# Input projection of a two-branch layer: seven block products of 2x2 blocks, in sweeps over pairs of column tiles

## Chip, core and metric

The kernel runs on one core of a Trainium2 chip. The metric is the device time of one execution in microseconds. In what follows PE is TensorE's matmul side, PEld its weight loads, DVE VectorE, ACT ScalarE, POOL GpSimd, SP SyncE (here it only issues DMAs).

## What is computed

One layer with two token mixers over a prompt of 1024 tokens and 8 samples of 8 tokens (1088 token columns), model width 2048, in float32:

```python
mod = silu(c) @ w_ada + b_ada
shift, scale, gate = split(mod, 3)
h = rms_norm(x, norm_gain) * (1 + scale) + shift
u_a, z_a, q, k, v, z_b, g_lr, m_a, m_b = split(h @ w_in, SPLIT_POINTS)
a_y, sa_re, sa_im = s5_branch(u_a, ...)          # diagonal complex state space, then a gated product with w_glu
a_out = (a_y * silu(z_a)) @ w_a_out
log_a = log_sigmoid(g_lr @ w_gate_up + b_gate) / 16
b_y, s_gla = gla_branch(q * DK ** -0.5, k, v, log_a, s0, head_gain)   # gated linear attention (GLA)
b_out = (b_y * silu(z_b)) @ w_b_out
merged = sigmoid(m_a) * a_out + sigmoid(m_b) * b_out
y = rms_norm(x + gate * (merged @ w_out), final_norm_gain)
```

`h @ w_in` is the input projection: 2048 rows by 72 column tiles of 128, and 16 further columns for `g_lr`.

## The kernel before

Activations lie with channels on partitions and tokens in the free dimension, as 16 k tiles of [128, 1088]. Every float32 operand of a large product is split into two parts (hi, lo), and a product is three matmuls: hi by hi, hi by lo, lo by hi (`mm3`, L69 to L71). Weights come in quarters of 4 k tiles, [128, 512]: SP loads the raw quarter (L52), ACT makes hi (L54), DVE makes lo (L56); six buffers each of hi and lo.

`product` (L73) walks the column tiles. For each of three token chunks (320, 384, 384 columns) it does 16 k steps of three matmuls into one PSUM bank and then calls an eviction function. Within it, `next(self.steps)` emits a piece of background work: first all of S5 (`s5_run`, L568: a setup of small DVE operations, then 16 units), later all of the GLA (`gla_run`, L733: four units of samples, 16 units of prompt). Evictions read PSUM on ACT (L601, L635, L644, L656), so the projection asks DVE for nothing but lo.

The program starts with the conditioning product (`ada_chunk`, L183: 16 chunks of 2 MB of `w_ada`), the norm of x, and `modulate` (L245), which gives hi and lo of h for one k tile; all 32 tiles of h then stay in SBUF until the projection is over. The first three column tiles go side by side over k (`product_k`, L91), two k tiles at a time, as soon as those two tiles of h are there, between the ada chunks. S5 runs beside column tiles 3 to 7 and those that follow, the GLA beside tiles 40 to 71, and eight last ada chunks (`ada_gates`, L956, with buffers of their own) beside tiles 8 to 15 and 32 to 39. Then come `branch_a` (w_glu), `merge` (w_a_out and w_b_out) and `final` (w_out).

The order in which each engine gets its instructions is set when the program is built: the framework's scheduler takes what the generators emit and orders each engine's queue by a simulated timeline. On the chip each queue runs in that order. A prompt unit of the GLA (`gla_unit`, L756) is one long chain: log gates (ACT with changes of its function table, DVE scans), seven levels of decays and scores (L814 to L842), the outputs and the state update (L932 to L941), and the norm (L945 to L953) with a DVE reciprocal (L133). Its scratch tile `t1` has one buffer: the norm at the end of a unit uses it, and so does the first step of the next unit (L778).

## Time and profile before

| | |
|---|---|
| time, median of 3 runs (range) | 2951.68 us (2951.25 to 2954.08) |
| span of the profiled execution | 2947.8 us |
| PE busy | 98% |
| DVE, ACT, POOL busy | 46%, 32%, 9% |
| granted TensorE clock, mean | 0.994 of full |
| DMA | 376.59 MB, mean 128 GB/s |

The page gives one profiled execution, engine by engine; a PE that is busy need not be at its peak, since matmuls overlap in the record. The run's own times lie 3.5 to 6.3 us above the profiled span (the median 3.9 us above). Busy shares are means over stages with different limits, so the stages are read by windows.

### The profile page before, as it was taken

How to read it: one execution, taken by the hardware profiler on the slowest of the kernel's cores; microseconds unless marked ns; L12 is line 12 of the kernel's file. 1: busy time of each engine (PE TensorE's matmuls, PEld its weight loads, DVE VectorE, ACT ScalarE, POOL GpSimd, SP SyncE). 2: the span in 40 equal slices, each digit the busy share in tenths (PEclk: the TensorE clock that was granted, in tenths of full speed). 3: DMA queues.
4: the chain of work that ended last, by engine and by line, in shares of the span. 5: the costliest groups of instructions: out<-in, count | busy, mean ns of one | idle time of the engine just before them, and what ended most of it. 6: DMA issues, size and time to landing. Idle time of an engine off the chain costs nothing.

```text
span 2947.8 us, 49487 instructions
## 1 busy us (share of the span) xinstructions
PE 2890.1 (98%) x19584; PEld 2762.2 (94%) x19584; DVE 1344.5 (46%) x3424; ACT 941.1 (32%) x1735; POOL 263.4 (9%) x430
## 2 busy tenths in 40 slices
PE   7999999999999999999999999999999999999988
PEld 3799999999989999999999999999999999899988
DVE  3587778751234444444453111114662233556455
ACT  4222222222234434443443111422232111444434
POOL 0002122210000000000000000301010000203021
PEclk9999999999999999999999999999999999999999
DMA  9634444442232222222223344423274333555455
GB/s 377 242 117 122 120 128 117 128 123 75 85 126 100 84 83 72 85 80 77 81 86 105 98 146 132 115 76 102 97 231 136 112 114 116 191 164 181 145 173 168
DMA packets 221881, 376.59 MB, mean 128 GB/s; under 512 B 35153, under 2 KB 111729, under 8 KB 219473
## 3 DMA queue, kind: packets, MB, share of 16 engines
q1 hardware_dynamic: 159856, 256.26, 26.8%
q0 software_dynamic: 24720, 75.59, 8.4%
q10 hardware_dynamic: 37072, 41.59, 4.1%
q8 instruction: 154, 2.52, 0.3%
q14 instruction: 79, 0.64, 0.1%
HBM read 288.44 MB, written 76.51 MB: 124 GB/s over the span
## 4 chain that ended last, share of the span: by engine, by line
PE 67%; DMA 2%; DVE 1%; ACT 1%; issue 1%; POOL 0%; DVEq 0%; ACTq 0%; POOLq 0%
PE mm L71 20%; PE mm L69 20%; PE mm L70 20%; DMA wraw<-in_w_out_dram 1%; DMA bz<-zbs 1%; PE bg L831 1%; PE bg L69 1%; PE bg L71 1%; PE bg L70 1%; PE bg L201 1%; PE bg L939 0%; PE bg L940 0%; PE bg L932 0%; DMA mx<-mscr 0%; DVE wlo L56 0%
## 5 line engine op out<-in xcount | busy, mean ns | idle before, releaser
L69 PE MATMUL mm<-hh,whi 128*128 128x384 f32 (+1 forms) x3360 | 1101.3, 329 | 4.2 <-ACT hh L264 4.2
L71 PE MATMUL mm<-hh,wlo 128*128 128x384 f32 (+2 forms) x3360 | 1103.0, 329 | 0.0
L70 PE MATMUL mm<-hl,whi 128*128 128x384 f32 (+1 forms) x3360 | 1100.0, 328 | 2.4 <-DVE hl L266 2.4
L56 DVE TENSOR_TENSOR wlo<-wraw,whi 128x512 fp32r<-128x512 f32 x560 | 406.1, 729 | 634.7 <-ACT whi L54 627.2
L69 PEld LDWEIGHTS mm<-hh,whi 128*128 128x128 f32 x3360 | 630.5, 188 | 19.2 <-issue 10.0
L70 PEld LDWEIGHTS mm<-hl,whi 128*128 128x128 f32 x3360 | 630.6, 188 | 10.1 <-DVE hl L266 3.6
L71 PEld LDWEIGHTS mm<-hh,wlo 128*128 128x128 f32 x3360 | 630.5, 188 | 5.5 <-issue 2.8
L54 ACT ACTIVATE whi<-wraw 128x512 fp32r<-128x512 f32 x560 | 351.3, 630 | 771.8 <-PE mm L70 561.6
L69 PE MATMUL mm<-ahi,whi 128*128 128x384 f32 (+3 forms) x1656 | 542.0, 328 | 13.4 <-DVE y L1084 10.4
L71 PE MATMUL mm<-ahi,wlo 128*128 128x384 f32 (+3 forms) x1656 | 542.2, 328 | 2.9 <-DVE wlo L56 2.9
L70 PE MATMUL mm<-alo,whi 128*128 128x384 f32 (+3 forms) x1656 | 541.6, 327 | 0.0
L69 PEld LDWEIGHTS mm<-ahi,whi 128*128 128x128 f32 x1656 | 313.5, 189 | 17.1 <-issue 11.0
L71 PEld LDWEIGHTS mm<-ahi,wlo 128*128 128x128 f32 x1656 | 313.5, 189 | 4.8 <-DVE wlo L56 3.5
L70 PEld LDWEIGHTS mm<-alo,whi 128*128 128x128 f32 x1656 | 313.6, 189 | 1.1
L635 ACT ACTIVATE ev<-mm 128x384 f32<-128x384 f32 (+1 forms) x120 | 55.9, 466 | 237.4 <-PE mm L71 234.4
L1042 DVE TENSOR_TENSOR m<-m,mm 128x384 f32<-128x384 f32 (+1 forms) x96 | 50.5, 529 | 146.9 <-PE mm L71 146.9
L645 DVE TENSOR_TENSOR ev<-ev,mm 128x384 f32<-128x384 f32 (+1 forms) x45 | 23.8, 530 | 181.3 <-ACT ev L644 181.2
L946 POOL TENSOR_TENSOR on<-on 128x256 f32<-128x256 f32 (+1 forms) x20 | 13.1, 653 | 961.3 <-ACT on L945 961.3
L644 ACT ACTIVATE ev<-mm 128x384 f32<-128x384 f32 (+1 forms) x45 | 21.1, 468 | 176.5 <-PE mm L71 176.3
L1040 ACT ACTIVATE m<-m 128x1088 f32<-128x1088 f32 x32 | 35.6, 1113 | 119.3 <-DMA m<-mbs 91.3
L480 POOL DMA_DIRECT2D tm<-kd x128 | 65.0, 516 | 43.0 <-DMA kd<-kk 18.8
L991 POOL DMA_DIRECT2D yt<-y x64 | 34.1, 540 | 380.1 <-ACT m L207 259.6
(334 smaller groups left out, 2580.6 us busy)
## 6 DMA issues: line engine op xcount, KB each, us to landing
wraw<-in_w_in_dram SPq DMA_DIRECT2D x288, 256.0 KB
wraw<-in_w_out_dram SPq DMA_DIRECT2D x192, 256.0 KB
adaraw<-in_w_ada_dram SPq DMA_DIRECT2D x64, 512.0 KB
gateraw<-in_w_ada_dram SPq DMA_DIRECT2D x16, 1024.0 KB
x<-in_xT_dram SPq DMA_DIRECT2D x16, 544.0 KB
m<-mas POOLq DMA_DIRECT2D x16, 544.0 KB, 4.9
m<-mbs POOLq DMA_DIRECT2D x16, 544.0 KB, 5.0
mscr<-m POOLq DMA_DIRECT2D x16, 544.0 KB, 3.1
```

The lines of the kernel that those rows point to most:

```text
L54: nc.scalar.activation(hi, raw, AF.Copy)
L56: nc.vector.tensor_tensor(lo, raw, hi.bitcast(F32), ALU.subtract)
L69: nc.tensor.matmul(ps, hi[:, c], ah[:, sl], start=start, stop=False)
L70: nc.tensor.matmul(ps, hi[:, c], al[:, sl], start=False, stop=False)
L71: nc.tensor.matmul(ps, lo[:, c], ah[:, sl], start=False, stop=stop)
L201: self.nc.tensor.matmul(ps[i:i + 32, :256], self.c32[:, k, :], raw[:, (k - k0) * 256:(k - k0 + 1) * 256], start=k < 4, stop=k >= KT - 4, t ...
L480: nc.gpsimd.dma_start(tm[16 * s:16 * s + 16], kd[0:16, :, 16 * (7 - s):16 * (7 - s) + P])
L635: nc.scalar.activation(e[:, :n], ps[:, :n], AF.Copy, scale=scale)
L831: nc.tensor.matmul(o, gs, blk(gs, w)[:, :, m:w], start=True, stop=True, tile_position=(0, 32 * i))
L991: nc.gpsimd.dma_start(yv[r:r + 16], self.yscr[2 * i + uu][:, g, :].rearrange("(t h) c -> h t c", h=16))
L1040: nc.scalar.activation(st["m"], st["m"], AF.Sigmoid)
L1042: V.tensor_tensor(mm, mm, ps[:, :n], ALU.mult)
```

## The change

The product of a pair of column tiles is written in 2x2 blocks: two halves of the k range, the two column tiles of the pair, and two halves of the tokens (544 each), and done with seven block products instead of eight (Winograd's form of Strassen's scheme). `SWEEPS` names the left operand (weights, or sums and differences of weight blocks) and the right operand (h, or sums and differences of blocks of h). 36 pairs stand in four groups of nine; within a group the kernel sweeps seven times over the nine pairs, one product per pair and sweep. Here one product of one pair is called a slot: 8 k tiles, two halves of 272 columns, three matmuls each, into two PSUM banks; there are two such buffers of two banks.

- Left operands (`left`): SP loads [128, 1024] blocks (tag `raw`, five buffers); for s1 to s4 POOL adds or subtracts two blocks; s1 and s2 are also written to DRAM and read back. ACT makes hi, DVE lo (three buffers each).
- Right operands: seven sets of 8 tiles, kept in DRAM. The first set and the second are made at the start (`blocks_first`, `blocks_second`), t1 too; t2, t3, t4 and 22 in the first group, as background (`blocks_sums`). Each further sweep reads its 8 tiles from DRAM (`right`), one per slot, into 16 buffers (two sets).
- Results: the first sweep's product goes to a tile by ACT; in all others DVE adds PSUM to it, once or twice per slot (288 additions of 544 columns). Finished quarters leave through four buffers (`fin`) by POOL's queue.
- Start: the ada chunks come first as a whole, then the sweeps. Background work: `blocks_sums` in the first group; then `behind`: S5 with one step per slot, the GLA with three, and `ada_gates`, whose raw tiles now come from the five `raw` buffers that the weight blocks use.

```diff
+    SWEEPS = (("a11", "11"), ("a12", "21"), ("s1", "t1"), ("s2", "t2"), ("s3", "t3"), ("a22", "t4"), ("s4", "22"))
+    def left(self, w, a, pair, scr):
...
+            raw = self.wx.tile([P, H], F32, tag="raw", name="araw", bufs=5)
+            nc.sync.dma_start(raw, src)
...
+        def both(x, y, op):
+            nc.gpsimd.tensor_tensor(x, x, y, op)
+            return x
...
+        elif a == "s1":
+            x = both(blk(j2, 0), blk(j2, 1), ALU.add)
+            nc.gpsimd.dma_start(scr[0], x)
+        elif a == "s2":
+            x = both(load(scr[0]), blk(j1, 0), ALU.subtract)
+            nc.gpsimd.dma_start(scr[1], x)
+        elif a == "s3":
+            x = both(blk(j1, 0), blk(j2, 0), ALU.subtract)
+        else:
+            x = both(blk(j1, 1), load(scr[1]), ALU.subtract)
+        hi = self.wi.tile([P, H], F32R, tag="whi", name="ahi", bufs=3)
+        nc.scalar.activation(hi, x, AF.Copy)
+        lo = self.wi.tile([P, H], F32R, tag="wlo", name="alo", bufs=3)
+        nc.vector.tensor_tensor(lo, x, hi.bitcast(F32), ALU.subtract)
...
+    def sweep_group(self, w, group, first, last, tail=None):
...
+        for r, (an, bn) in enumerate(self.SWEEPS):
...
+            for i, (pair, s, final) in enumerate(group):
+                hi, lo = self.left(w, an, pair, self.sscr[pair])
+                ps = self.psum2()
+                for k in range(8):
+                    c = slice(k * P, (k + 1) * P)
+                    for m in range(2):
+                        o = ps[:, m, :NC]
+                        bh, bl = B[k][:, m * NC:(m + 1) * NC], B[k][:, HT + m * NC:HT + (m + 1) * NC]
+                        nc.tensor.matmul(o, hi[:, c], bh, start=k == 0, stop=False)
+                        nc.tensor.matmul(o, hi[:, c], bl, start=False, stop=False)
+                        nc.tensor.matmul(o, lo[:, c], bh, start=False, stop=k == 7)
+                    if k in self.ticks:
+                        next(self.steps, None)
+                next(coming, None)
...
+                if r == 0:
+                    nc.scalar.activation(two(x), v, AF.Copy, scale=s)
+                elif r == 1:
+                    out(0, 0, x)
+                elif r == 2:
+                    add(y, x)
+                elif r == 3:
+                    add(x, x)
+                    add(y, y)
+                elif r == 4:
+                    add(x, x)
+                    out(1, 1, y)
+                elif r == 5:
+                    out(1, 0, x, -1)
+                else:
+                    out(0, 1, y)
...
-            for k in range(0, KT, 8):
-                raw = self.gp2.tile([P, 2048], F32, tag="raw", name="gateraw", bufs=3)
...
+            for k in range(0, KT, 4):
+                raw = self.wx.tile([P, 1024], F32, tag="raw", name="gateraw", bufs=5)
...
+    def behind(self):
+        self.s5ctx = ExitStack()
+        self.ticks = (3,)
+        yield from self.s5_run()
+        self.s5ctx.close()
+        self.ticks = (1, 4, 6)
+        gla = ExitStack()
+        self.gla_pool(gla)
+        yield from self.gla_run()
+        gla.close()
+        yield from self.ada_gates()
...
+        self.ticks = (2, 5)
+        self.steps = self.blocks_sums()
+        for g in range(4):
+            self.sweep_group(w, pairs[9 * g:9 * g + 9], g == 0, g == 3)
+            if g == 0:
+                for _ in self.steps:
+                    pass
+                su.close()
+                self.steps = self.behind()
+                next(self.steps)
```

What the change moves on the engines' queues stands below at three places (names as in the trace: `mm` is a product's PSUM tile, `bg` one of the background work).

**PE, start.** Before, among the ada chunks (L201) the first column tiles (L69 to L71) already run:

```order
L201 MATMUL bg<-adaraw,c_210 32x256 x12
L69 MATMUL mm<-hh,whi 128x384
L69 MATMUL mm<-hh,whi 128x320
L201 MATMUL bg<-adaraw,c_210 32x256 x4
L70 MATMUL mm<-hl,whi 128x384
L71 MATMUL mm<-hh,wlo 128x384
```

With the change (ada is L336 and L344, the sweeps are L167 to L169):

```order
L344 MATMUL bg<-ident,m 128x128 x2
L336 MATMUL bg<-adaraw_1148,c_283 32x256 x4
L336 MATMUL bg<-adaraw_1154,c_283 32x256 x4
L336 MATMUL bg<-adaraw_1160,c_283 32x256 x4
L344 MATMUL bg<-ident,m 128x128 x2
L167 MATMUL mm<-b_543,ahi 128x272
L168 MATMUL mm<-b_543,ahi 128x272
L169 MATMUL mm<-b_543,alo 128x272
```

Every ada matmul now stands ahead of the first matmul of the projection.

**PE, GLA.** Before, where one prompt unit ends (L949) and the next begins (L775), projection matmuls stand on both sides, and so at each step of each unit:

```order
L69 MATMUL mm<-hh,whi 128x320
L70 MATMUL mm<-hl,whi 128x320
L949 MATMUL bg<-on,ones_h 128x256
L775 MATMUL bg<-gr,wgu 128x256
L801 MATMUL bg<-q,k 32x32 x8
L71 MATMUL mm<-hh,wlo 128x320
L69 MATMUL mm<-hh,whi 128x320
```

With the change, at the end of the sixth sweep of the last group (L1163 ends a unit, L989 begins one):

```order
L167 MATMUL mm<-bt_22230,ahi 128x272
L168 MATMUL mm<-bt_22230,ahi 128x272
L169 MATMUL mm<-bt_22230,alo 128x272
L1163 MATMUL bg<-on,ones_h 128x256
L989 MATMUL bg<-gr,wgu 128x256
L1015 MATMUL bg<-q,k 32x32 x8
L1045 MATMUL bg<-g 32x16 x40
L1054 MATMUL bg<-g 32x32 x4
L1054 MATMUL bg<-g 64x64 x2
L1086 MATMUL bg<-ident,kd 128x128 x2
L1146 MATMUL bg<-v,kT 128x256 x2
```

Seven whole prompt units stand there one behind the other with no matmul of a sweep between them; the last of them and the first matmuls of the seventh sweep:

```order
L1154 MATMUL bg<-q,St_16190 128x128
L1163 MATMUL bg<-on,ones_h 128x256
L336 MATMUL bg<-gateraw,c_283 32x256 x16
L344 MATMUL bg<-ident,m 128x128 x2
L336 MATMUL bg<-gateraw,c_283 32x256 x8
L167 MATMUL mm<-b_22455,ahi 128x272
L168 MATMUL mm<-b_22455,ahi 128x272
```

Before those seven, the prompt units stand among the sweeps, about six slots to a unit. On SP's queue the second weight block that the seventh sweep's first pair needs stands behind the loads and stores of the same seven units.

**DVE, S5's setup.** Before, no eviction of the projection is on DVE. With the change, in the second sweep of the second group, the addition of the first pair's product (L187) is followed by 157 rows of S5 (its setup, the tables and scans of its first units) and three of lo, and then by that of the second pair; the end of the stretch:

```order
L693 TENSOR_TENSOR rt<-rot,par 128x8
L694 TENSOR_TENSOR rot<-rot,rt 128x4x2
L695 TENSOR_TENSOR rot<-rot,rt 128x4x2
L691 TENSOR_TENSOR rot<-rot,par 128x8x4
L692 TENSOR_TENSOR rt<-rot,par 128x16
L693 TENSOR_TENSOR rt<-rot,par 128x16
L694 TENSOR_TENSOR rot<-rot,rt 128x4x4
L187 TENSOR_TENSOR fin<-pt,mm 128x544
```

Before, rows of this kind stand between two of lo, and no matmul waits for them; now an addition that frees a PSUM buffer stands behind them.

## Rows read from the trace of the kernel before

**Rows 1.** The page: busy time of each engine, and the chain that ended last.

```profile
PE 2890.1 (98%) x19584; PEld 2762.2 (94%) x19584; DVE 1344.5 (46%) x3424; ACT 941.1 (32%) x1735; POOL 263.4 (9%) x430
...
PE 67%; DMA 2%; DVE 1%; ACT 1%; issue 1%; POOL 0%; DVEq 0%; ACTq 0%; POOLq 0%
```

**Rows 2.** Busy time by windows (us, PE, PEld, DVE, ACT, POOL busy, PE clock, DMA share, GB/s).

```profile
10.00:20.00 10.00, 10.00 (x46) 3.75 (x45) 0.00 (x0) 8.32 (x8) 0.00 (x0) 1.00 1.02 415
...
400.00:500.00 100.00, 100.00 (x661) 98.09 (x660) 77.26 (x295) 22.73 (x53) 22.36 (x44) 1.00 0.43 127
1200.00:1400.00 200.00, 200.00 (x1680) 192.79 (x1668) 88.77 (x259) 79.71 (x172) 3.68 (x5) 1.00 0.25 79
```

**Rows 3.** PE timeline, 384 columns (start, length, what).

```profile
1699.41 0.33 PE L69 MATMUL mm<-hh,whi 128*128 128x384 f32 x1
...
1700.28 0.34 PE L71 MATMUL mm<-hh,wlo 128*128 128x384 f32 x1
```

**Rows 4.** PE timeline, 320 columns.

```profile
1702.10 0.31 PE L69 MATMUL mm<-hh,whi 128*128 128x320 f32 x1
...
1703.26 0.31 PE L71 MATMUL mm<-hh,wlo 128*128 128x320 f32 x1
```

**Rows 5.** PE timeline, 256 columns.

```profile
2871.73 0.28 PE L71 MATMUL mm<-ahi,wlo 128*128 128x256 f32 x1
...
2872.91 0.28 PE L69 MATMUL mm<-ahi,whi 128*128 128x256 f32 x1
```

**Rows 6.** Line L69 on PE, to 200 us (ns min/median/max, first and last start).

```profile
L69 PE MATMUL bg<-hh,whi x48: 358/368/496, 59.5 to 168.7; 128*128 128x448 f32 x32, 128*128 128x512 f32 x16
```

**Rows 7.** DMA issues of the page's sixth part (count, KB each).

```profile
adaraw<-in_w_ada_dram SPq DMA_DIRECT2D x64, 512.0 KB
...
x<-in_xT_dram SPq DMA_DIRECT2D x16, 544.0 KB
```

**Rows 8.** Lines L71 and L775 on PE, 1200 to 1400 us.

```profile
L71 PE MATMUL mm<-hh,wlo x344: 307/334/444, 1200.1 to 1399.9; 128*128 128x384 f32 x116, 128*128 128x320 f32 x56
...
L775 PE MATMUL bg<-gr,wgu x5: 468/471/471, 1228.5 to 1395.3; 96*128 96x256 f32 x5
```

**Rows 9.** ACT timeline, the start of one prompt unit.

```profile
1233.33 0.46 ACT L778 ACTIVATE t<-bg 128x256 f32<-128x256 f32 x1
...
1236.83 0.51 ACT L780 ACTIVATE t<-t,one 128x256 f32<-128x256 f32 x1
```

**Rows 10.** DVE timeline, the norm of one unit.

```profile
1229.47 1.74 DVE L133 RECIPROCAL rsn<-t 128x256 f32<-128x256 f32 x1
...
1232.95 0.69 DVE L953 TENSOR_TENSOR on<-bg,rsn 128x512 f32<-128x512 f32 x1
```

**Rows 11.** DVE and ACT groups by shape (busy us, mean ns, idle before them).

```profile
L814 DVE TENSOR_TENSOR d<-b 128x256 f32<-128x256 f32 x112 | 43.5, 418 | 0.5
L1042 DVE TENSOR_TENSOR m<-m,mm 128x384 f32<-128x384 f32 x64 | 35.1, 551 | 113.2 <-PE mm L71 113.2
L817 DVE TENSOR_TENSOR g<-d,k 128x128 f32<-128x128 f32 x112 | 31.8, 284 | 0.0
...
L1046 DVE TENSOR_TENSOR m<-m 128x1088 f32<-128x1088 f32 x16 | 20.5, 1283 | 0.0
...
L815 ACT ACTIVATE d<-d 128x128 f32<-128x128 f32 x112 | 34.3, 306 | 17.2 <-DVE d L814 17.1
```

**Rows 12.** Lines L1131 and L977 on DVE and POOL (ns min/median/max, first and last start).

```profile
L1131 POOL TENSOR_TENSOR y<-y,rs x12: 1982/2438/2777, 2691.4 to 2850.0; 128x832 f32<-128x832 f32 x12
L1131 DVE TENSOR_TENSOR y<-y,bg x6: 677/678/686, 2938.4 to 2941.4; 128x512 f32<-128x512 f32 x6
L1131 DVE TENSOR_TENSOR y<-y,rs x4: 1026/2808/2814, 2691.3 to 2843.1; 128x832 f32<-128x832 f32 x4
...
L1131 POOL TENSOR_TENSOR y<-y,rc x2: 1263/1264/1264, 2938.4 to 2939.6; 128x512 f32<-128x512 f32 x2
...
L977 DVE TENSOR_TENSOR alo<-mx,ahi x11: 1276/1278/4007, 2511.5 to 2549.3; 128x1088 fp32r<-128x1088 f32 x11
```

More of the change, by code (lines that the diff above doesn't have):

```diff
@@ L29 @@
 QK4 = 512
+HT = T // 2
+NC = HT // 2
 class Hybrid:
@@ L234, in norm_in @@
-        tmp = self.act(F32, "rt")
-        for c, (t0, n) in enumerate(CH):
-            part = self.ep.tile([P, 416], F32, tag="ev", name="part", bufs=3)
-            nc.scalar.activation(part[:, :n], pss[c][:, :n], AF.Copy)
-            pss[c] = self.psum(False)
-            nc.tensor.matmul(pss[c][:, :n], ones_32, part[:, :n], start=True, stop=True)
-            nc.scalar.activation(tmp[:, t0:t0 + n], pss[c][:, :n], AF.Ln, bias=self.eps)
+            if k < KT // 2:
+                nc.scalar.activation(sq, self.x[k], AF.Square)
+            else:
+                for h in range(2):
+                    nc.scalar.activation(sq[:, h * HT:(h + 1) * HT], parts[k][h], AF.Square)
@@ new lines, in norm_in @@
+            for h in range(2):
+                for c in range(2):
+                    o = h * HT + c * NC
+                    nc.tensor.matmul(pss[h][i:i + 32, c, :NC], self.ones_d[:, 0:32], sq[:, o:o + NC],
+                                     start=k < 4, stop=k >= KT - 4, tile_position=(0, i))
+        self.rs = sp.tile([P, T], F32, name="rs")
+        tmp = self.pt(F32, "rt")
+        part = self.pt(F32, "part")
+        for h in range(2):
+            o = h * HT
+            two = lambda x: x[:, o:o + HT].rearrange("p (c n) -> p c n", c=2)
+            nc.scalar.activation(two(part), pss[h][:, :, :NC], AF.Copy)
+            pss[h] = self.psum2()
+            for c in range(2):
+                nc.tensor.matmul(pss[h][:, c, :NC], ones_32, part[:, o + c * NC:o + (c + 1) * NC], start=True, stop=True)
+            nc.scalar.activation(two(tmp), pss[h][:, :, :NC], AF.Ln, bias=self.eps)
@@ new lines, in glr @@
+    def glr(self, r, B):
+        nc = self.nc
+        ps = self.psum2()
+        k0 = 8 if r in (1, 6) else 0
+        for k in range(8):
+            for m in range(2):
+                for p in range(2):
+                    nc.tensor.matmul(ps[0:32, m, :NC], self.w2[:, k0 + k, :], B[k][:, p * HT + m * NC:p * HT + (m + 1) * NC],
+                                     start=k + p == 0, stop=k + p == 8)
+        two = lambda t: t.rearrange("p (c n) -> p c n", c=2)
+        v = ps[0:32, :, :NC]
+        g = self.gsum
+        if r == 0:
+            for h in range(2):
+                nc.scalar.activation(two(g[:, h, :]), v, AF.Copy)
+            return
+        h = 0 if r == 1 else 1
+        nc.vector.tensor_tensor(two(g[:, h, :]), two(g[:, h, :]), v, ALU.add)
+        if r == 2:
+            return
+        e = self.su.tile([96, HT], F32R, tag="ge", name="ge")
+        ef = e.bitcast(F32)
+        nc.scalar.activation(e[0:32], g[:, h, :], AF.Copy)
+        nc.scalar.activation(e[64:96], g[:, h, :], AF.Copy)
+        nc.vector.tensor_tensor(e[32:64], g[:, h, :], ef[0:32], ALU.subtract)
+        nc.scalar.dma_start(self.ga[:, h * HT:(h + 1) * HT], ef)
@@ L1170, in run @@
[L1170 to L1180 removed]
+        self.glr_load()
@@ new lines, in raws @@
+        def raws(early):
+            while True:
+                if early:
+                    yield self.pt(F32, "adaraw")[:, :1024]
+                    yield self.pt(F32, "adaraw")[:, :1024]
+                yield self.wx.tile([P, 1024], F32, tag="raw", name="adaraw2", bufs=5)
+        r = raws(True)
+        for j in range(4):
+            self.ada_chunk(j, r)
+            self.ada_chunk(8 + j, r)
+            for k in (2 * j, 2 * j + 1):
+                self.blocks_first(k)
+        r = raws(False)
@@ L1199, in run @@
-        ev = self.evict_silu(rows(32, self.zbs))
-        self.product(w, range(32, 38), h, ev)
-        self.product(w, [38, 39], h, ev, kouter=True)
-        for _ in self.gates:
-            pass
-        gates.close()
+        wctx.close()
+        pmm.close()
+        self.pmm = self.pool("pmm2", space=PSUM)
+        self.ap2 = self.pool("acts2")
+        self.wp = self.pool("weights")
+        self.nact = 0
+        self.homes = ["op"] * 8 + ["pt"] * 8 + ["op"] * 8 + ["pt"] + ["ap"] * 7
         self.p2ctx = ExitStack()
```

390 lines of the change are left out of this document (231 added, 159 removed).

## The prediction

> **What bounds the kernel now.** I read the busy shares first: PE 2890.1 of 2947.8 us, DVE and ACT far below [rows 1]. The chain that ended last is PE for 67%, and no other engine has more than 2% of it [rows 1]. By windows PE has no idle time at all in the projection, both beside S5 (400 to 500 us) and beside the GLA (1200 to 1400 us), at the full granted clock [rows 2]. So before, every matmul column removed is time saved, and every wait that PE does not have now is time lost. The sum is made against the profiled execution: its span is 2947.8 us, and the median of the runs, 2951.68, lies 3.9 us above; I add 4 us at the end.
>
> What a matmul takes is its pitch, start to start, not its recorded length (they overlap): 384 columns 0.174 us (0.87 over 5 steps) [rows 3], 320 columns 0.145 (1.16 over 8) [rows 4], 256 columns 0.118 (1.18 over 10) [rows 5]. It goes with the columns and has no part that a narrower matmul pays again. 272 columns lie a quarter of the way from 256 to 320: 0.125 us.
>
> **The change, part by part.**
>
> *The seven products.* Before, one column tile costs 48 x (0.145 + 2 x 0.174) = 23.7 us. The first three tiles' last matmul stands at 168.7 us [rows 6], and 69 tiles are left: 1635 us. Now there are 36 pairs x 7 = 252 slots of 48 matmuls: 252 x 48 x 0.125 = 1512 us, 6.0 us a slot. That is **-123**.
>
> *The start.* No sweep matmul stands ahead of the last conditioning matmul. Until then x, w_ada [rows 7] and 32 stores of right operands have to move, 16 x 0.557 + 64 x 0.524 + 32 x 0.557 = 60.3 MB. The best stretch of the trace moves 415 GB/s, with every DMA engine busy [rows 2]: 60.3 MB take 145 us at that, and with some 15 us until the stream runs the sweeps begin at about 160 us, against 168.7 for the 69 tiles: **-9**. Bounds: 145 and 185 (DMA idle a fifth of the time).
>
> [...]
>
> *The GLA's last units.* On PE's queue seven prompt units stand between two slots with no sweep matmul among them, so PE goes at the pace of their chain. A unit is one chain because of t1: the next unit's first step on ACT (L778 before) waits for the last Newton step of the norm, which reads it. From the trace: the start on ACT, two table loads among it, 4.0 us (1233.33 to 1237.34) [rows 9]; DVE's log gate and scans, some 1.2; seven levels in a row, each DVE 0.42, ACT 0.31, DVE 0.28 [rows 11] and a small matmul, 1.2, so 8.4; state, output and decays about 3; the square, its matmul, the table load and root about 3; the norm on DVE 3.5 (1229.47 to 1232.95) [rows 10]; some 25 hand-overs of 0.08. That is about 25 us a unit. PE's own work of a unit was paid before too: in 200 busy us PE did 3 x 344 sweep matmuls at 0.164, 169 us, and the units' share is 31 us at 41.7 us a unit (1228.5 to 1395.3 are four) [rows 8], 6.4 a unit. So 7 x (25 - 6.4) = **+130**. Bounds: DVE's own sum over a unit, 18.2 us by the means of its rows (L814 the largest [rows 11]) less a tenth of overlap (below), 16.4, gives +70; the pace of before, 41.7, gives +247. I take the chain, as nothing stands between its links any more and 41.7 is a pace that slots set. The sweep's next weights do not hide it: they stand behind the units' loads on SP.
>
> *S5's setup.* In the second sweep of the second group 157 DVE rows of S5 stand between two additions. At their means of before they are 49.5 us; overlap between neighbours takes a tenth off (DVE's groups add to 1501 by mean and count, to 1344.5 on the page [rows 1]): 44. PE has the slot it is in and the second pair of banks, 12 us, then waits: **+32**. Bounds: 0, if the rows come earlier than the slot (they can run as soon as the first addition is done, and PE may be late itself), and 50.
>
> *Additions and lo on DVE, and POOL's sums.* An addition of 544 columns is worth 0.71 us from 384 columns at 0.551 [rows 11], lo of 1024 columns 1.2 from 1088 at 1.28 [rows 12]. With 1.14 additions a slot DVE has 2.0 us of 6.0: beside the GLA (88.8 of 200 us now [rows 2], half of it lo) covered. Beside S5 it is not loose: lo, additions and S5's rows of a sweep come to about 52 us against 54 to 60 of PE. There POOL's sums of 1024 columns come in, 2.4 us each (832 columns 2.44, 512 columns 1.26, [rows 12]). Beside POOL the DVE's subtraction of two SBUF tiles took 2.81 us at most where 1.03 was the least, and 4.0 against 1.28 [rows 12]; the one with an operand in PSUM took 0.68 every time [rows 12]. Nine sums a sweep in four of seven sweeps, some 0.6 us lost each where DVE is the bound: **+6** for each of six sweeps beside S5, **+35** in all. Bounds: 0, and the whole length of each sum (below).
>
> *Transfers.* In the third sweep of the first group two weight blocks, a store, a right tile and the building of the next right tiles make about 3.3 MB a slot, more than 6 us carry at 415 GB/s (2.5 MB): **+10** (bounds 0 and 18). In the last sweep the gates' weights go through the same five raw buffers as the sweep's blocks, some 45 loads, 23.6 MB or 57 us beside 54 of PE: **+20** (0 and 57). The turn to the gated product, for which pools are closed and opened: **+8** (0 and 20). Elsewhere a slot moves some 1.5 MB, 260 GB/s: covered. ACT's hi of 1024 columns takes 1.1 us a slot, POOL's sums 2.4: covered.
>
> *Sum.* -123 - 9 + 130 + 32 + 35 + 10 + 20 + 8 = +103: span 3051, time **3055 us**.
>
> **The rivals.**
>
> *A, faster: the units run at DVE's pace and the small waits are hidden.* For it: ACT's start and the norm of neighbouring units could overlap where the trace leaves their order free. Against it: t1's single buffer. Then 2948 - 132 + 70 + 32 + 4 = 2922 us. It decides for faster where the seven units cost under 18 us each and the additions wait for nothing beside S5. Chance 0.15.
>
> *B, POOL holds DVE for each whole sum.* 4.0 us in place of 1.28 and 2.81 in place of 1.03 [rows 12] speak for it; that most rows of that group keep 1.28 speaks against. Then 2.4 us x 9 in each of six sweeps, of which about 14 us is beyond PE's time: 84 in place of 35, and 10 more beside the GLA: 3055 + 59 = 3114 us. Chance 0.08. [...]
>
> *C, the seven units go at the pace of before*, 41.7 us [rows 8], since their steps wait for loads, table loads and DMA returns that I took as hidden: 3055 + 7 x 16.7 = 3172 us. Chance 0.10.
>
> *D, a matmul of 272 columns costs what one of 320 does*, 0.145: 252 x 48 x 0.02 = 242 us more, 3297 us. The pitches of rows 3 to 5 speak against it. Chance 0.02. [...]
>
> **How the numbers follow.** About 0.2%, 6 us, is what a measurement of this kernel can tell from no change. My forecast has 0.62, A 0.15, B 0.08, C 0.10, D 0.02, and 0.03 lies within 6 us of no change. So faster 0.15, same 0.03, slower 0.82. The forecast's own range is 2990 to 3120 (the units between 20 and 30 us each, -35 to +35, and the small waits between nil and their bounds). The range takes in A and B and most of C: 2910 to 3180.
>
> **What would show it.** Right: the first sweep matmul at about 160 us; slots of 6.0 us with PE at full clock where nothing else stands; one stretch of about 175 us ahead of the last sweep in which PE is mostly idle, behind ACT and DVE in turn; an idle of some 30 us in the second group's second sweep, released by L187; short idles beside S5 that end with DVE. Wrong: slots over 6.3 us with PE busy (the pitch); no idle stretch before the last sweep (the order on PE is then no guide to the pace); units of under 18 us in it; idle ended by DMA in most slots (then transfers bound the sweeps, and the time is above the range).

## The result and the profile after

The changed kernel takes 3236.55 us (median of 4 runs, 3230.05 to 3244.16) against 2951.47 (4 runs): a ratio of 1.0967, with a 95% interval of 1.095 to 1.0985. It is slower, as forecast, but by 285 us and not by 103; the time lies 57 us above the stated range (2910 to 3180). The profiled execution has a span of 3242.4 us (its own time is 3244.16).

The page after: busy time, granted clock in 40 slices, and the chain that ended last. The first and the third line answer to [rows 1]; the clock of the page before follows.

```profile
PE 2821.3 (87%) x21384; PEld 2670.8 (82%) x21384; DVE 1851.8 (57%) x3673; ACT 1047.2 (32%) x1652; POOL 855.9 (26%) x846
...
PEclk8599999979989999999999999557799999999999
...
PE 42%; DMA 7%; DVE 7%; issue 5%; ACT 4%; POOL 2%; SPq 0%; POOLq 0%; DVEq 0%; ACTq 0%
```

```profile
PEclk9999999999999999999999999999999999999999
```

PE has fewer busy microseconds than before (2821 against 2890) and a longer span: it was idle for 13%. The clock, at 90% or more of full speed in every slice before, dips in many. PE's share of the last chain fell from 67% to 42%, and DMA, DVE, "issue" and ACT took up most of the rest.

By windows (columns as in [rows 2]): the first group of sweeps; the slot in which S5's setup stands; the rest beside S5; beside the GLA; the seven units that stand alone; the last sweep.

```profile
155.00:601.00 446.00, 410.91 (x3172) 404.58 (x3173) 218.61 (x221) 109.25 (x134) 162.10 (x110) 0.95 0.83 292
...
667.00:725.00 58.00, 18.73 (x123) 16.47 (x122) 36.27 (x151) 6.79 (x17) 11.85 (x19) 0.62 0.35 109
725.00:1414.00 689.00, 624.70 (x4904) 611.08 (x4904) 525.03 (x1254) 149.68 (x255) 277.77 (x287) 0.95 0.79 258
1414.00:2008.00 594.00, 564.88 (x5074) 537.65 (x5073) 374.52 (x757) 267.91 (x442) 180.77 (x143) 0.97 0.68 237
2008.00:2214.00 206.00, 86.53 (x1060) 66.52 (x1059) 115.76 (x356) 92.42 (x196) 11.98 (x13) 0.62 0.13 44
2214.00:2333.00 119.00, 85.89 (x606) 73.23 (x610) 42.00 (x38) 39.50 (x35) 66.15 (x85) 0.79 0.75 223
```

The projection's own pace is what was forecast. Two rows of PE's timeline, nine matmuls apart, with nothing else on PE:

```profile
500.95 0.29 PE L169 MATMUL mm<-bt,alo 128*128 128x272 f32 x1
...
502.07 0.29 PE L169 MATMUL mm<-bt,alo 128*128 128x272 f32 x1
```

1.12 us for nine is 0.124 us for 272 columns (0.125 was worked out from [rows 4, 5]). The sweeps begin here (L167 on PE, first start):

```profile
L167 PE MATMUL mm<-b,ahi x1728: 283/287/597, 154.9 to 2332.4; 128*128 128x272 f32 x192
```

154.9 us, where 160 was forecast. So neither the products nor the start are at fault. What was lost lies between 155 and 2333 us. I split it by the matmul records and the record of the granted clock: time in which no matmul runs ("idle"), and half of the busy time at the lower of the record's two levels, 1.00 and 0.50 of full ("clock").

What the lower level costs is seen at the second sweep's start, behind an idle of 7.9 us; the window's granted clock is 0.50 of full (its third column from the end). Two rows of PE, nine matmuls apart:

```profile
226.00:229.00 3.00, 2.85 (x12) 2.85 (x13) 1.28 (x2) 2.70 (x5) 0.00 (x0) 0.50 1.04 361
```

```profile
226.15 0.59 PE L167 MATMUL mm<-b,ahi 128*128 128x272 f32 x1 [7.90 <-ACT pt L196]
226.54 0.43 PE L168 MATMUL mm<-b,ahi 128*128 128x272 f32 x1
...
228.59 0.43 PE L168 MATMUL mm<-b,ahi 128*128 128x272 f32 x1
```

2.05 us for nine is 0.228 us a matmul, against 0.124: 1.83 times as long, so 0.45 of the busy time at that level is lost there. So the table's half is somewhat high; if all matmuls went as these do, the 107 us of its clock column would be 97.

| stretch (the windows above; us) | forecast | idle | clock | lost |
|---|---|---|---|---|
| first group | 10 | 35 | 14 | 49 |
| slot of S5's setup | 32 | 39 | 5 | 44 |
| rest beside S5, 601 to 667 and 725 to 1414 | 35 | 64 | 21 | 85 |
| beside the GLA | 0 | 29 | 19 | 48 |
| seven units alone | 130 | 119 | 31 | 150 |
| last sweep | 20 | 33 | 18 | 51 |
| sum | 227 | 320 | 107 | 427 |

In the projection of before, by the same reckoning, 5 us are lost in 1881. PE's waits over the whole span, after (what waited, for whom; us in total, times, longest):

```profile
PE bg L1045 <- DVE g L1032: 110.2, 35, 12.4
PE mm L167 <- ACT ahi L130: 30.5, 10, 8.0
...
PE mm L169 <- DVE alo L132: 27.0, 13, 7.0
...
PE bg L667 <- DVE bm L652: 20.9, 1, 20.9
PE bg L764 <- DVE rot L685: 19.6, 3, 17.4
PE mm L167 <- DVE pt L187: 18.7, 8, 5.7
```

The largest is the GLA's (L1045 is a level's scores, L1032 the product before it). The lines with `mm` are waits of the sweeps for hi and lo of the weights and for additions. L667 and L764 are matmuls of S5 itself; their longest waits, 20.9 and 17.4 us, are the slot of S5's setup. PE's queue runs in the program's order, so a background matmul that is not ready holds up the sweep's matmuls behind it. Beside the GLA (1414 to 2008 us, first lines) all 29 us of PE's idle time end at such matmuls, and beside S5 (725 to 1414 us, the two largest lines of PE's waits there) some 26 of 64 us:

```profile
PE bg L1045 <- DVE g L1032: 23.4, 14, 4.9
PE bg L1163 <- POOL on L1160: 5.0, 3, 3.3
```

```profile
PE mm L167 <- DVE pt L187: 14.2, 6, 5.7
PE bg L871 <- DVE fin L187: 12.7, 4, 9.6
```

### The profile page after: what moved, and what is told of

Read it like the earlier page. It is cut to its first block, busy times and chain, and to the rows that moved or that the text cites. A ratio compares the mean times of both kernels' runs of the same rounds, so it can differ in the third digit from the quotient of the medians.

```text
span 3242.4 us, 54558 instructions
## 1 busy us (share of the span) xinstructions
PE 2821.3 (87%) x21384; PEld 2670.8 (82%) x21384; DVE 1851.8 (57%) x3673; ACT 1047.2 (32%) x1652; POOL 855.9 (26%) x846
## 4 chain that ended last, share of the span: by engine, by line
PE 42%; DMA 7%; DVE 7%; issue 5%; ACT 4%; POOL 2%; SPq 0%; POOLq 0%; DVEq 0%; ACTq 0%
PE mm L71 7%; PE mm L73 7%; PE mm L72 7%; PE mm L169 5%; PE mm L167 5%; PE mm L168 5%; DMA araw<-in_w_in_dram 3%; POOL araw L111 1%; DVE alo L132 1%; DMA bz<-zbs 1%; DMA araw<-s 1%; DMA yt<-y 1%; DMA wraw<-in_w_out_dram 1%; DVE g L1031 1%; PE bg L1146 1%
## 5 line engine op out<-in xcount | busy, mean ns | idle before, releaser
L167 PE MATMUL mm<-bt,ahi 128*128 128x272 f32 x2304 | 680.2, 295 | 44.2 <-DVE pt L187 18.7
L169 PE MATMUL mm<-bt,alo 128*128 128x272 f32 x2304 | 679.0, 295 | 15.0 <-DVE alo L132 15.0
L168 PE MATMUL mm<-bt,ahi 128*128 128x272 f32 x2304 | 675.3, 293 | 0.0
L71 PE MATMUL mm<-ahi,whi 128*128 128x384 f32 (+3 forms) x1656 | 543.7, 329 | 10.9 <-DVE y L1311 8.0
L167 PE MATMUL mm<-b,ahi 128*128 128x272 f32 x1728 | 511.0, 296 | 29.8 <-ACT ahi L130 16.7
L130 ACT ACTIVATE ahi<-araw 128x1024 fp32r<-128x1024 f32 x252 | 266.4, 1058 | 819.6 <-PE mm L168 447.3
L169 PE MATMUL mm<-b,alo 128*128 128x272 f32 x1728 | 510.8, 296 | 12.0 <-DVE alo L132 12.0
L168 PE MATMUL mm<-b,ahi 128*128 128x272 f32 x1728 | 506.6, 293 | 0.0
L167 PEld LDWEIGHTS mm<-bt,ahi 128*128 128x128 f32 x2304 | 447.9, 194 | 50.4 <-issue 26.4
L111 POOL TENSOR_TENSOR araw<-araw 128x1024 f32<-128x1024 f32 x144 | 372.4, 2587 | 433.9 <-DMA araw<-in_w_in_dram 278.1
L169 PEld LDWEIGHTS mm<-bt,alo 128*128 128x128 f32 x2304 | 446.0, 194 | 18.8 <-DVE alo L132 17.0
L168 PEld LDWEIGHTS mm<-bt,ahi 128*128 128x128 f32 x2304 | 445.3, 193 | 2.4 <-issue 1.2
L132 DVE TENSOR_TENSOR alo<-araw,ahi 128x1024 fp32r<-128x1024 f32 x252 | 348.7, 1384 | 114.4 <-ACT ahi L130 114.0
L167 PEld LDWEIGHTS mm<-b,ahi 128*128 128x128 f32 x1728 | 337.5, 195 | 36.3 <-ACT ahi L130 18.9
L169 PEld LDWEIGHTS mm<-b,alo 128*128 128x128 f32 x1728 | 335.8, 194 | 18.1 <-DVE alo L132 15.5
L168 PEld LDWEIGHTS mm<-b,ahi 128*128 128x128 f32 x1728 | 335.3, 194 | 0.7 <-issue 0.2
L71 PEld LDWEIGHTS mm<-ahi,whi 128*128 128x128 f32 x1656 | 314.2, 190 | 15.8 <-issue 8.7
```

Of the source, the lines that this page charges most:

```text
L71: nc.tensor.matmul(ps, hi[:, c], ah[:, sl], start=start, stop=False)
L111: nc.gpsimd.tensor_tensor(x, x, y, op)
L130: nc.scalar.activation(hi, x, AF.Copy)
L132: nc.vector.tensor_tensor(lo, x, hi.bitcast(F32), ALU.subtract)
L167: nc.tensor.matmul(o, hi[:, c], bh, start=k == 0, stop=False)
L168: nc.tensor.matmul(o, hi[:, c], bl, start=False, stop=False)
```

## The experiments

Each run is one execution with its profile. The kernel before, run beside each, took 2948 to 2956 us, and the four runs of the changed kernel lie 14 us apart, so differences of some 15 us between totals are not read as anything.

**1. All background behind the sweeps (bare).**

```diff
         for g in range(4):
+            if g:
+                self.ticks = ()
             self.sweep_group(w, pairs[9 * g:9 * g + 9], g == 0, g == 3)
```

> All of S5, of the GLA and of the gates is emitted behind the last sweep; the sweeps are as in the changed kernel, and the first group keeps its background. Theory 1 (the sweeps supply themselves; the excess comes from background rows on queues that run in order, and from the lower clock behind each idle): sweeps of groups two to four take 54 to 55 us each, 21 of them 1140 us against 1731 now, PE idle under 1% and the clock at 1.00 there; the first group stays near 447 us. Theory 2 (weights, POOL's sums and DVE's lo and additions hold the sweeps back by themselves): the mean of those sweeps stays over 60 us. The whole is longer by some hundreds of us in either case, since the background then runs alone.

Measured: 3633.9 us. The sweeps of groups two to four take 1151 us, with 10 us idle; the first group 448. The sweeps end at 1754.8 us. By windows, the third group's sweeps and then the GLA alone; and the first matmul of each GLA unit (L989):

```profile
997.00:1377.00 380.00, 377.49 (x3021) 377.30 (x3021) 141.36 (x135) 71.44 (x72) 118.22 (x90) 1.00 0.76 270
2140.00:2630.00 490.00, 192.71 (x2200) 138.69 (x2200) 267.15 (x902) 219.96 (x483) 11.37 (x18) 0.56 0.15 47
```

```profile
L989 PE MATMUL bg<-gr,wgu x20: 401/470/775, 2135.6 to 2632.0; 96*128 96x256 f32 x16, 96*128 96x64 f32 x4
```

Theory 1 holds: the sweeps feed themselves at 6.0 us a slot and at full clock, DMA share 0.76 and all. Alone, a unit takes 26.1 us (19 steps in 496.4 us, four of them of the samples), at a mean clock of 0.56. In the changed kernel, the units that stand alone:

```profile
L989 PE MATMUL bg<-gr,wgu x7: 467/468/775, 2018.2 to 2176.9; 96*128 96x256 f32 x7
```

Six steps in 158.7 us: 26.5 each. The prediction had 25.

This run also tells the pace of S5, by the first matmul of a unit (four a unit): before, after, and alone.

```profile
L466 PE MATMUL bg<-ident,bm x64: 271/272/328, 232.8 to 618.4; 128*128 128x128 f32 x64
```

```profile
L667 PE MATMUL bg<-ident,bm x64: 271/273/445, 694.3 to 1333.1; 128*128 128x128 f32 x64
```

```profile
L667 PE MATMUL bg<-ident,bm x64: 270/417/422, 1754.8 to 2105.7; 128*128 128x128 f32 x64
```

From the first to the last of these matmuls, some fifteen units, it is 386 us before, 639 after and 351 alone. Before, S5 starts at 233 us and is through when a good quarter of the column tiles are; now it starts at 694, since u is complete only when all seven sweeps of the first group are over, and goes at 42.6 us a unit. The GLA follows it. That is why seven units are left over; runs 7 to 10 agree, where S5 goes faster and at most two are left.

**2. The gates behind the sweeps (gates_last).**

```diff
         gla.close()
-        yield from self.ada_gates()
...
         for _ in self.steps:
             pass
+        for _ in self.ada_gates():
+            pass
```

> The gates' conditioning product is emitted behind the last sweep, so that its raw tiles no longer hold the five buffers while the GLA runs; nothing else is changed. Theory 1 (raw tiles held through the GLA keep the last sweep's weights out, so seven units run alone): the stretch of 199 us ahead of the last sweep is gone, two units run beside that sweep, five behind it at about 28 us each (140 us), then the gates for 35 to 45 us of DMA; sweep seven takes 75 us, not 119; total about 3175 us (3150 to 3200). Theory 2 (the GLA's chain puts the block there in any case): the block stays ahead of the last sweep and the time is within 20 us of 3237.

Measured: 3214.6 us, 22 less. The last sweep and what follows it, by windows:

```profile
2026.00:2100.00 74.00, 67.45 (x676) 64.79 (x675) 50.65 (x102) 46.78 (x76) 31.91 (x23) 0.93 0.42 137
2100.00:2304.00 204.00, 89.30 (x949) 55.37 (x949) 94.66 (x287) 78.50 (x157) 23.70 (x41) 0.59 0.37 108
```

The block is gone from its place and the last sweep takes 73 us, as theory 1 says: the raw tiles held it there. But the time went from there to 2100 to 2304 us: five units and the gates, 204 us where 175 to 185 were expected. So the buffers decide where the left-over units stand, not what they cost. The expected total was missed by 15 us, on the side of a smaller gain.

**3. Without POOL's sums (no_pool_sums).**

```diff
         def both(x, y, op):
-            nc.gpsimd.tensor_tensor(x, x, y, op)
             return x
```

> POOL's additions and subtractions of weight blocks (s1 to s4, 144 of them) are left out, so the left operand of these sweeps is one block; both blocks are still loaded. Theory 1 (what I forecast: POOL's sums slow DVE by 35 us beside S5, and add their 2.4 us to the supply chain of a slot): lo's longest falls from 3.8 us to about 1.3, the sweeps beside S5 together get 35 to 70 us shorter, the first group 15 to 30; total 3140 to 3190. Theory 2 (S5's own rows on DVE make those waits, POOL's sums are covered): under 20 us less.

Measured: 3099.6 us, 137 less, more than either theory. The kernel leaves out the 144 sums and still loads both blocks. The nine sweeps from 770 to 1394 us go from 624 to 576 us (48, in the range of theory 1), the first group only from 447 to 440, less than theory 1's 15 to 30; the rest lies in later stretches: one unit less in the block (six), 10 us of idle beside the GLA and not 29, and a last sweep without POOL in its supply. Lo beside S5 (L132 after, L131 here), and DVE there by windows, after (this window runs 20 us past the nine sweeps) and here:

```profile
L132 DVE TENSOR_TENSOR alo<-araw,ahi x84: 1195/1220/3774, 768.3 to 1408.2; 128x1024 fp32r<-128x1024 f32 x84
```

```profile
L131 DVE TENSOR_TENSOR alo<-araw,ahi x82: 1197/1218/1226, 763.0 to 1337.2; 128x1024 fp32r<-128x1024 f32 x82
```

```profile
770.00:1414.00 644.00, 582.90 (x4578) 569.97 (x4577) 486.14 (x1143) 138.92 (x232) 253.80 (x260) 0.95 0.79 261
```

```profile
762.00:1339.00 577.00, 552.65 (x4423) 545.35 (x4424) 389.76 (x1111) 128.91 (x209) 105.59 (x201) 0.98 0.85 280
```

Most lo's are not touched (median 1.22 us either way); the longest is 3.77 us with the sums and 1.23 without. DVE is busy for 486 us with them and 390 without. The rows of the changed kernel show how a sum costs DVE time; the longest lo, and the sum on POOL beside it:

```profile
851.78 3.77 DVE L132 TENSOR_TENSOR alo<-araw,ahi 128x1024 fp32r<-128x1024 f32 x1
```

```profile
852.07 2.40 POOL L111 TENSOR_TENSOR araw<-araw 128x1024 f32<-128x1024 f32 x1
```

The lo ends at 855.55 us, 1.08 us behind the sum's end (854.47), close to the 1.22 us that a lo takes with no sum beside it: I read its record as a wait for the sum and then its work. From 770 to 1414 us 44 rows of DVE are more than 0.15 us longer than the median of their kind, and every one of them ends within 1.1 us behind the end of a sum. The stretch has 55 sums; 12 of them cost DVE nothing, and the 55 together some 86 us, 1.6 us each. My term had 0.6.

**4. S5's setup early (setup_early).**

```diff
-        self.s5_setup()
...
-        self.steps = self.blocks_sums()
+        self.steps = itertools.chain(self.blocks_sums(), self.s5_setup())
```

(and some fifteen `yield` in `s5_setup`, with scratch tiles shared).

> S5's setup is emitted in pieces from the end of the first group's third sweep on, two pieces a slot, and no longer at the start of the second group. Theory 1 (the addition behind 157 rows costs what PE waits there): the slot of 57 us in the second group's second sweep falls to under 10 us, and the time by 45 to 50 us, to about 3190. Theory 2 (S5's units are what DVE is late with, so the wait moves on): the slot is shorter, but later sweeps take up more than half of it; less than 25 us off.

Measured: 3191.8 us, 45 less, the total of theory 1. The second group's second sweep, after and here:

```profile
655.00:770.00 115.00, 72.53 (x545) 69.58 (x545) 86.33 (x295) 20.49 (x44) 35.82 (x47) 0.79 0.56 177
```

```profile
686.00:757.00 71.00, 62.85 (x490) 61.89 (x490) 50.06 (x125) 17.75 (x33) 22.44 (x31) 0.95 0.77 229
```

PE is idle for 42 us of the one and 8 of the other; the sweep's longest slot falls from 57 us to 15, not to under 10. But the 45 us are not the price of that slot alone. The first group, where the pieces stand now, takes 470 us and not 447 (its fifth sweep 69 us, not 55); the second group 482 and not 531; the last 712 and not 743, since S5 and the GLA start sooner and six units are left for the block, not seven. That the total came out at 45 is in part chance.

What PE waited for in the slot is seen in its rows and DVE's (after):

```profile
694.27 1.08 PE L667 MATMUL bg<-ident,bm 128*128 128x128 f32 x4 [20.85 <-DVE bm L652]
...
715.95 0.79 PE L764 MATMUL bg<-X,ca 128*128 128x136 f32 x2 [17.38 <-DVE rot L685]
```

```profile
688.95 0.17 DVE L691 TENSOR_TENSOR rot<-rot,par 128x8 f32<-128x8 f32 x1 [6.04 <-DMA par<-s5par]
...
723.28 0.71 DVE L187 TENSOR_TENSOR fin<-pt,mm 128x544 f32<-128x544 f32 x1
```

PE's idle time ends at the first unit's own matmuls (L667, L764), which stand on PE's queue ahead of the sweep's next. The addition (L187), which the forecast had PE wait for, ends at 724.0 us, and the sweep's next matmul starts at 724.6; so the addition would have held PE about as long, but no wait there ends with it. Between this addition and the one before it, 61 us, DVE was busy for only 40. The longest stop is from 676 to 689 us, in which S5's parameters are stored to DRAM and read back.

**5. The first group's stores on POOL's queue (first_group_stores).**

```diff
-                t = sp.tile([P, T], F32, tag="t", name="st", bufs=2)
+                t = sp.tile([P, T], F32, tag="t", name="st", bufs=1)
...
-                    st = sp.tile([P, T], F32R, tag="st", name="st2", bufs=2)
+                    st = sp.tile([P, T], F32R, tag="st", name="st2", bufs=3)
...
-                    nc.scalar.dma_start(self.oscrp[name][k], st.bitcast(F32))
+                    nc.gpsimd.dma_start(self.oscrp[name][k], st.bitcast(F32))
```

> In the first group the stores of the right operands that are built there (t2, t3, t4, 22) are issued by POOL's queue and no longer by ACT's, into three buffers (the tile that they are built from has one). Theory 1 (ACT's queue runs in order: its stores wait for DVE's lo of the same tile, and the eviction of the projection and the next hi stand behind them): the first group falls from 447 us to 405 to 425, time 3195 to 3215. Theory 2 (the first group is short of DMA, or waits for POOL's sums): under 10 us off, and PE's idle time there stays near 35 us.

Measured: 3206.7 us, 30 less; the first group takes 426 us, 21 less, 20 of them idle. Theory 1, at the small end. The edit changes the queue and the number of buffers together; which of the two gains how much is not shown. What it removes is seen on ACT's timeline after, at the end of the first sweep (ACTq is its queue):

```profile
213.06 0.33 ACTq L469 DMA_DIRECT2D opt<-st  x1
...
218.79 1.15 ACT L460 ACTIVATE sx<-sx,mod 128x1024 f32<-128x1024 f32 x1 [3.79 <-DVE sx L407]
...
223.33 2.10 ACTq L469 DMA_DIRECT2D opt<-st  x2
225.48 0.62 ACT L196 ACTIVATE pt<-mm 128x544 f32<-128x544 f32 x1 [4.45 <-DVE st L418]
```

The two stores (L469) can only be issued when DVE's lo of their tile (L418) is done, the second at 225 us; the eviction of the sweep's product (L196) and the next hi (L130) stand behind them. PE's 7.9 us of idle ahead of 226.15 us (above) end with that eviction, and the slot takes 18 us.

**6. The sums on DVE (sums_on_dve).**

```diff
-            nc.gpsimd.tensor_tensor(x, x, y, op)
+            nc.vector.tensor_tensor(x, x, y, op)
```

> The 144 sums of weight blocks are done by DVE and no longer by POOL. Theory 1 (a sum on POOL holds up DVE's operations on two SBUF tiles for about 1.4 us of its 2.4, as the run without the sums suggests: beside S5 DVE was busy 486 us with them and 390 without, 61 sums apart): DVE pays 1.2 us for a sum and no longer 1.4, and the weights are ready 1.2 us sooner; the sweeps beside S5 get 15 to 45 us shorter, lo's longest is 1.3 us, total 3160 to 3215. Theory 2 (what the sums cost is work, wherever it is done, or DVE's order is what holds PE): total 3230 or more, with more idle time released by DVE.

Measured: 3157.2 us, 79 less. The nine sweeps beside S5 take 588 us (36 less, in the range), the last sweep 90 and not 119, lo's longest is 2.37 us and not the 1.3 expected. Theory 1, and 3 us beyond its range. That the wait of a slot for POOL counts too fits the shorter last sweep, but was not tested by itself.

**7 to 10. All together.** combo has S5's setup early, one gate chunk per sweep beside S5, and

```diff
-        yield from self.s5_run()
+        for i, _ in enumerate(self.s5_run()):
+            if i % 5 != 4:
+                yield
...
-        t1, b = new("t1")[:, :n], new("b")[:, :n]
+        t1, b = new("t1", bufs=2)[:, :n], new("b")[:, :n]
```

> S5's setup early (as in that run), the eight gate chunks one per sweep beside S5 and not behind the GLA, five steps of S5 in four slots, so that the GLA begins some 19 slots sooner, and two buffers for the scratch tile t1. Theory 1 (S5 and the GLA are one chain behind the first group, and what of it is left when the sweeps end runs alone at 26.5 us a unit): no block before the last sweep, last sweep under 75 us, one unit or two left behind it; the sweeps end at about 2130 us, total 3040 to 3090. Theory 2 (the chain's pace beside the sweeps falls as far as its start moves forward): several units are left, and the total stays above 3130.

Measured: 3106.4 us. No block ahead of the last sweep (69 us), one unit behind it, but the sweeps end at 2142 us, and a gate chunk costs more than I had put: in each of the four sweeps of the second group that need sums two slots take 13 to 26 us. The mechanism is theory 1's, the total 16 us above its range. What each of the four edits gave by itself is not shown.

combo_all is combo with the edits of runs 5 and 6.

> The run before, with the sums on DVE and the first group's stores on POOL's queue as well. If the three costs are separate ones, their gains add up: combo less 20 to 40 us for the stores and 15 to 45 for the sums, 2960 to 3050, PE idle in the projection under 80 us. If DVE is what all three run into, the total is within 20 us of combo.

Measured: 3044.5 us, 62 less than combo, in the range for separate costs, though runs 5 and 6 alone took off 30 and 79. The projection is idle for 110 us, not under 80.

combo_b3 and combo_b4 move the chunks and speed up S5's steps (`i % 3 != 2` and `i % 4 != 3`):

```diff
+                if not first and r in (0, 1, 5) and i in (2, 6):
+                    next(self.gates, None)
```

> As combo_all, with the gate chunks moved out of the sweeps that need sums or two blocks into those with one block (first, second and sixth sweep, two chunks each), and S5 at three steps in two slots, so that the whole GLA stands beside the sweeps. Theory 1 (what is left of combo_all's excess is the 80 us between the last sweep and the next product, in which two units run alone, and some 40 us at the gate chunks): total 2940 to 2985, no prompt unit behind the last sweep, the gate slots under 10 us. Theory 2 (DVE is full beside S5, so that a faster S5 only moves the wait into its sweeps): the sweeps of the second group get longer by as much as the tail gets shorter, total above 3010.

> As combo_b3, with S5 at four steps in three slots. One unit is left behind the last sweep. Theory 1: 10 to 30 us slower than combo_b3 for that unit (26.5 us) and the wait for w_glu behind it. Theory 2: faster than combo_b3, since S5 presses less on DVE.

Measured: 3013.1 and 3065.8 us. No unit is left behind the sweeps in combo_b3, and the best time of all, but 28 us above the expected range, and 2% slower than before. Its page, the second group's fifth sweep by windows with PE's largest wait in it, and the 22 us behind the last sweep:

```profile
PE 2753.5 (91%) x21384; PEld 2622.0 (87%) x21384; DVE 1822.6 (61%) x3817; ACT 1040.6 (35%) x1652; POOL 506.0 (17%) x734
```

```profile
PE bg L779 <- DVE rot L700: 42.8, 2, 25.0
```

```profile
876.00:996.00 120.00, 75.73 (x598) 73.32 (x596) 93.86 (x308) 20.63 (x44) 25.03 (x48) 0.82 0.62 193
2088.00:2110.00 22.00, 4.60 (x21) 4.38 (x20) 6.80 (x9) 9.17 (x10) 19.06 (x34) 0.59 0.90 200
```

Where S5's steps are emitted faster than its units go, several units stand in a row on PE and DVE: one slot of 66 us. That is theory 2's mechanism, and the total lies in its range too: against combo_all the time behind the last sweep falls by 84 us, from 1006 to 922, but the second group's sweeps take 563 us and not 517, and all sweeps 52 us more. combo_b4 loses 53 us to combo_b3, more than the 10 to 30 for one unit left over. All of it lies behind the last sweep: its sweeps end at 2085.6 us, 3 before those of combo_b3, and 978 us follow, not 922, with one unit and a wait of 28.7 us of the next product among them.

**11. Matmuls that only keep PE busy (warm_block).**

```diff
             for i in range(4, len(units)):
-                yield from unit(i)
+                for _ in unit(i):
+                    if i > 12:
+                        pw = self.psum(False)
+                        for _ in range(5):
+                            nc2.tensor.matmul(pw, self.wgu[:, :P], self.wgu, start=True, stop=True)
+                    yield
```

> Behind every step of the seven prompt units that run alone, five matmuls of 512 columns are added, whose result nobody reads (420 in all, 90 us at full clock). Theory 1 (the lower clock behind PE's idle time lengthens the units: PE's 6.4 us of a unit take 12.8 at half clock, and they are links of its chain): the clock in the block rises from 0.62 to over 0.9, the units fall from 26.5 us to 21 to 24, the block gets 15 to 35 us shorter in spite of the added matmuls. Theory 2 (the links are DVE's, ACT's and the hand-overs): units stay at 26 us or get longer by what the added matmuls stand in the way.

Measured: 3342.3 us, 106 more. (The 90 us for the 420 matmuls are low: at the 0.23 us from start to start that 512 columns took at full clock, before, L69 to L71 from 124.06 us on, they are some 97 us.) Theory 1 fails: the units get longer, as theory 2 has it for matmuls that stand in the way. The block by windows:

```profile
2000.00:2300.00 300.00, 233.91 (x1452) 168.65 (x1451) 112.59 (x354) 88.98 (x193) 10.83 (x13) 0.68 0.07 23
```

The mean clock is 0.68, where 0.62 stood without; units take 41 us. The added matmuls stood in the way of the units' own, at the lower clock for most of the time (a mean of 0.68 between 1.00 and 0.50 is 0.64 of it). What the clock alone costs such a chain is thus not shown by a run; the split above rests on the records of matmuls and clock.

**12. The gate chunks in the first group (combo_c3).**

```diff
-                if not first and r in (0, 1, 5) and i in (2, 6):
+                if first and r > 3 and i in (1, 4, 7):
```

> As combo_b3, with the gate chunks in the first group's last three sweeps, where nothing else runs beside, so that none stands beside S5. Theory 1 (a gate chunk between weight blocks costs PE some 5 to 10 us where DVE and DMA are busy with S5): the second group's sweeps get 20 to 45 us shorter in all, the first group's last three 10 to 20 longer; total 2975 to 3005. The slot of 66 us in the second group's fifth sweep, where three units of S5 stand in front of a transpose of v, remains. Theory 2 (a chunk costs the same everywhere): within 10 us of combo_b3.

Measured: 3058.1 us, 45 more than combo_b3. The second group's sweeps get 13 us shorter in all, the first group's last three take 234 us and not 170. Neither theory: there the chunks stand among the pieces of S5's setup and the blocks of v, and cost 64 us. combo_b3 stays the best.

## Why the prediction was wrong in size

*The products and the start* were right: 12,096 matmuls at 1.12 us for nine are 1505 us (forecast 1512), and the start is at 154.9 us (160). With these, S5's, the GLA's and the gates' own matmuls and no loss, the projection would take some 1750 us, against 1881 before.

*The GLA's seven units* were read rightly from the order of rows: they stand alone, at 26.5 us a unit (forecast 25), and cost 150 us (130). Run 2 shows what puts them there, run 1 that their chain sets the pace, and the S5 rows why so many are left. Rivals A (18 us) and C (41.7) fell: 42 us is the pace beside other work, 26 the pace alone.

*S5's setup* cost 44 us (forecast 32), and that the two are as near as this is partly luck. S5's rows on DVE do hold PE, and PE did work 12 us ahead. But the sign that was named, an idle released by L187, did not come: PE waited 38 us at S5's own matmuls (rows in run 4). And DVE was busy for 40 us, not 44; the 21 us in which it stood still between the two additions had no term.

*The first step that failed* is the sum's silence on TensorE's clock. Each term counted a wait of PE once, as time lost at full pace. In the trace the 320 us of idle go with some 214 us of matmuls at the lower level, which cost 107 us by the table. Of these 31 lie among the seven units, where the forecast's 25 us a unit stand for idle and matmuls together; the other 76 us had no term, though the prediction named the granted clock at 1.00 as a condition. The runs agree: with 110 us idle (combo_all) it is 31, with 10 us (bare, groups two to four) 3 or 4. The share differs by stretch: 5 us for 39 of idle in the slot of S5's setup, 19 for 29 beside the GLA. The table reckons half of the busy time at the granted clock of 0.50 as lost; the pitches measured at 226 and 501 us, 0.228 us against 0.124, make it 0.45.

*The second step that failed*, 103 us, is idle time at five terms that were too small. The forecast had PE wait for weights and additions, and for a background chain only where no sweep matmul stands; that a background matmul on PE's own queue holds the sweep behind it everywhere else had no term. (a) S5's setup, 39 for 32: above. (b) Beside the GLA, 29 for 0: lo and additions were covered, as forecast, and none of the idle ends with them; all of it stands ahead of the GLA's own matmuls (L1045, L1163). (c) Beside S5, 64 for 35: some 26 us are waits of background matmuls, the rest waits of the sweeps, most for DVE. A sum on POOL costs DVE 1.6 us and not 0.6; without the sums (run 3) PE is idle for 24 us in nine sweeps, where the window above has 61. (d) The first group, 35 for 10: I looked at the DMA alone; in run 5 stores on ACT's queue wait for DVE, with evictions and hi's behind them, and its edit takes 21 us off the group. (e) The last sweep, 33 for 20: gates and weights through the same buffers, with POOL's sums in the supply; run 6 takes 29 us off it.

*Rival B* was right in its mechanism: the long rows of DVE end behind a sum's end, one by one (run 3). The 1.6 us are a mean over 55 sums: 12 that cost DVE nothing, and 43 that met a row midway or held one from the start (lo by 0.3 to 2.55 us over its median of 1.22). For PE, B's price of 84 us was too high and the forecast's 35 too low: without the sums the nine sweeps are 48 us shorter.

The differences make up the miss: losses 200 over forecast (76 clock, 103 idle, 20 in the block of units), products -7, start -5, and the tail from the last sweep to the end at 909.8 us against 898.4 before, 3 more than the 8 put on: 191 of 3242.4 - 3051.

Rival D fell with the pitch: a matmul of 272 columns takes 0.124 us and not the 0.145 of 320, in proportion to its columns (0.453 to 0.461 ns a column in [rows 3, 4, 5], 0.457 here).

## What to carry to other kernels

Where PE is always busy, fewer matmul columns are worth their pitch only as long as nothing else that PE waits for moves with them: look first at when the background chains can start and whether they still fit beside what is left. Put something on top of PE's waits for the clock behind them: over the whole projection it was 0.28 of the idle in combo_all (31 of 110 us) and 0.33 in the changed kernel (107 of 320). Look for waits by the order in each queue, PE's own first, and not by busy shares: here waits of background matmuls, which hold up all that stands behind them, were all 29 us of PE's idle beside the GLA and some 26 of 64 beside S5. A rewrite that is 130 us shorter by its matmuls came to 285 us longer; with all that the runs taught it is still 60 us longer.

## What the runs showed of the hardware

A matmul of 272 columns has a pitch of 0.124 us at full clock and of 0.228 at a granted clock of 0.50: 1.83 times as long, not twice.

The same chain of a GLA unit takes 26 us alone at a mean clock of 0.56, and 41.7 us ([rows 8], before) or 35 to 54 us (prompt units, after) beside a stream of matmuls at a mean clock of 1.00 and 0.97. Beside the stream its steps stand where the program's order puts them, between slots; alone, at 0.56, it is still faster.

Filling PE's gaps did not bring the clock back: with PE busy 234 of 300 us in run 11 the mean granted clock was 0.68, with 86.5 of 206 it was 0.62.

From 770 to 1414 us of the changed kernel a sum of two SBUF tiles on POOL takes 2.4 us in the median, and 43 of 55 sums have a long DVE row that ends within 1.1 us behind them. It goes the other way too: 15 DVE rows on two SBUF tiles lie within the record of a sum, all in sums of 2.9 to 4.4 us, and each ends at least 2.2 us before the sum does; none ends in a sum's last 2.2 us. DVE's additions with an operand in PSUM are not touched there: 16 of them lie wholly within a sum, each 0.71 or 0.72 us long.
